# The last part of a decoder layer's down projection: the plain products of the last 256 rows, computed with rows on partitions instead of output features

## The chip, the cores and the metric

The kernel runs on one core of one Trainium2 chip. The metric is the device time of one execution in microseconds (us), the median of three runs. The matrix engine is PE, its weight loads are PEld, the vector engine is DVE, the scalar engine ACT, and SP issues the DMA transfers.

## The reference

One layer of a hybrid decoder is applied to 16 learned meta tokens and 512 prompt tokens, and to 8 separate sample tokens, with a model width D of 2048: a combined projection, windowed attention beside causal pooling, an output projection, a layer normalisation, a SwiGLU feed-forward part and a second normalisation. All inputs and outputs are float32. The change lies in the last three lines of it:

```python
def post_sublayers(h, attn_out, pool_out, w_o, ln1_g, ln1_b, w_gate, w_up, w_down, ln2_g, ln2_b):
    ...
    h1 = layer_norm(DEEPNORM_ALPHA * h + mix, ln1_g, ln1_b)
    a = jax.nn.silu(jnp.einsum('btd,df->btf', h1, w_gate)) * jnp.einsum('btd,df->btf', h1, w_up)
    ff = jnp.einsum('btf,fd->btd', a, w_down)
    return layer_norm(DEEPNORM_ALPHA * h1 + ff, ln2_g, ln2_b)
```

Here d_ff is 44 tiles of 128, and the normalisation takes mean and variance over the 2048 features of a token. The 8 sample rows and the 512 prompt rows are outputs; the meta rows are dropped.

## The kernel before, in words

*Layout.* A token is called a row here, as in the reference. Almost everywhere the kernel keeps features on the 128 partitions and tokens as columns. The sum alpha * h1 + ff thus stands in 16 tiles `acc[m]` of 128 features, each with 520 columns: 8 sample rows, then 512 prompt rows. At the very end it must be turned round, as a normalisation over the 2048 features of a row needs a row on one partition, and as the output is stored by rows.

*Arithmetic.* A float32 number is split into a rounded part and the rest, both in the type fp32r (`split`: ACT makes the high part in L187, DVE the low part in L188). Of each pair of operands PE makes three products (`products`, L203, L204 and L206: high by high, high by low, low by high). `rr` is the region of memory of such parts, `fr` that of float32 tiles. In a product the left operand is the stationary one (a tile of 128x128, loaded by PEld) and the right one moves through it column by column.

*The down projection.* Most of the 44 d_ff tiles go through a scheme of seven products instead of eight for pairs of blocks (`column_pair`); their sums stand in PSUM tiles `tri` and are added to `acc` by DVE (L1243 to L1256). Four d_ff tiles (f = 0 to 3, called `places`) are left out of that scheme and are done plainly at the end by `down(h, m)`. That is the stage the change touches. Its hidden activations are kept split as `ah[f]` and `al_[f]`, 128 features by 520 columns. For half h = 0 (264 columns: the sample rows and 256 prompt rows), and then for h = 1 (256 columns: the last 256 prompt rows), and for each of 16 output tiles m, there are 4 x 3 products with a 128x128 piece of w_down stationary and the columns moving, into a bank `d`; DVE adds the bank to `acc[m]` (L1336). So there are 192 products a half. The weights come in four loads of 4 tiles m (L1328, two buffers `pl`), and are split once for each m, with all four f side by side, 512 columns.

*Turning and normalising.* The 512 prompt rows are four blocks of 128, `Rows` 0 to 3; blocks 0 and 1 belong to the first half, 2 and 3 to the second. After every fourth m, `Rows.part(q)` turns 4 tiles of each block of the half by PE transposes with an identity matrix (L1350) into a bank `tz`, four to a bank: 16 banks and 64 transposes for the four blocks. ACT copies the bank to a tile `z` (L1352), and DVE takes statistics of its 512 features (L1354). After four parts, `Rows.end` aggregates them (L250), makes one over the standard deviation (`rstd_of`, L236 to L242, with the root on ACT in L237), and makes for each quarter q a centring pass (L1361: subtract the mean, times the weight) and a scaling pass (L1363: times one over the deviation, plus the bias), each over 128x512 on DVE. The scaled quarter is stored (L1364). The passes of blocks 0 and 1 are issued among the products of the second half; those of blocks 2 and 3 come after all of PE's products.

*The sample rows* are normalised without turning, by `sample_rows`, a generator advanced at fixed places: `tg` turns the norm's weights (L1378), column sums are made by products with a matrix of ones (L1392, tiles `zm` and `zv`), DVE scales (L1401 to L1403), and one last transpose `to` (L1406) brings the 8 x 16 pieces into rows, which ACT copies (L1408) and 16 small DMAs store (L1411).

*What sets the order.* A tile scheduler puts the instructions of each engine into one fixed order by the order of the program and by what its own model says of readiness; rings of buffers (8 PSUM banks, the `pl` and `z` buffers) hold steps back. `step()` pins the order of the instructions inside it. At run time every engine works through its own list in order, so an instruction that waits holds all behind it on that engine.

Of the kernel before, what the change touches and what calls it, by code (L numbers as in the profile page):

```python
# [8 lines left out]
F32 = mybir.dt.float32  # L9
F32R = mybir.dt.float32r  # L10
AF = mybir.ActivationFunctionType
ALU = mybir.AluOpType
AX = mybir.AxisListType

P = 128
D = 2048
KT = D // P
SEQ = 512
META = 16
NS = 8  # L20
# [29 lines left out]
NZ = 19  # L50
# [17 lines left out]
def hybrid_step(ctx, tc, xin, w_in, w_o, w_g, w_u, w_d, w_pool, par_d, cst_d, ident_d, ln2gb, kct_d, vc_d, hist_d,  # L68
                ck_d, cv_d, sp_d, yp, ys, nkp, nvp, npp, nks, nvs, nps):
    nc = tc.nc  # L70
# [744 lines left out]
    def bank(name, w=HN):  # L815
        return ps.tile([P, 512], F32, tag="bank", name=name, bufs=banks)[:, :w]
# [490 lines left out]
    plp = Pool(fr)  # L1307
# [6 lines left out]
    pw, ws = {}, {}  # L1314
# [8 lines left out]
    def down(h, m):  # L1323

        if m % 4 == 0 and h == 0:
            pw[h] = plp.tile([P, 4, 4, P], F32, tag="pl", name=f"pl{h}_{m}", bufs=2)
            for f, (c, x) in enumerate(places):
                nc.sync.dma_start(pw[h][:, :, f, :], w_d[c, m:m + 4, :, x * P:(x + 1) * P].rearrange("m p c -> p m c"))  # L1328
        hs = DHALF[h]
        out = bank(f"d{h}_{m}", hs.stop - hs.start)  # L1330
        if h == 0:
            ws[m] = split(pw[h][:, m % 4], f"dp{m}")
        wh, wl = ws[m]
        for f in range(4):
            products([out], wh[:, f, :], wl[:, f, :], [ah[f][:, hs]], [al_[f][:, hs]], f == 0, f == 3)
        nc.vector.tensor_add(acc[m][:, hs], acc[m][:, hs], out)  # L1336
# [4 lines left out]
    class Rows:  # L1341
        def __init__(self, c0, n, dst):
            self.c0, self.n, self.dst, self.z = c0, n, dst, []
            self.st, self.mv = stats_tile(pb, f"z{c0}")

        def part(self, q):
            n, c0 = self.n, self.c0
            tp = bank(f"tz{c0}_{q}", 512)
            for i in range(4):
                nc.tensor.transpose(tp[:n, i * P:(i + 1) * P], acc[4 * q + i][:, c0:c0 + n], ident)  # L1350
            z = zp.tile([P, 512], F32, tag="z", name=f"z{c0}_{q}", bufs=NZ)[:n]
            nc.scalar.copy(z, tp[:n])  # L1352

            nc.vector.bn_stats(self.st[:n, q, :], tp[:n] if q == 3 else z)  # L1354
            self.z.append(z)

        def end(self):
            n = self.n
            mu, r = stats_end(pb, self.st, self.mv, n, f"z{self.c0}")
            for q, z in enumerate(self.z):  # L1360
                nc.vector.scalar_tensor_tensor(z, z, mu, gb[0][q][:n], op0=ALU.subtract, op1=ALU.mult)  # L1361
                yield
                nc.vector.scalar_tensor_tensor(z, z, r, gb[1][q][:n], op0=ALU.mult, op1=ALU.add)  # L1363
                nc.sync.dma_start(self.dst[:, q * 512:(q + 1) * 512], z)  # L1364
                yield
# [50 lines left out]
    rows = [Rows(NS + P * i, P, yp[P * i:P * (i + 1), :]) for i in range(4)]  # L1416
    for h, part in ((0, rows[:2]), (1, rows[2:])):
        for m in range(KT):
            down(h, m)
            if h == 1:  # L1420

                for _ in range(2 if m % 4 == 1 else 1):
                    next(ends, None)
            if h == 0 and m in (1, 2):
                for i, q in gb_loads[4 * m - 4:4 * m]:
                    nc.sync.dma_start(gb[i][q], ln2gb[i:i + 1, q * 512:(q + 1) * 512].to_broadcast([P, 512]))
            if m % 4 == 3:
                for x in part:
                    x.part(m // 4)
            if (h, m) in ((0, 4), (0, KT - 1), (1, 4), (1, 10), (1, KT - 1)):  # L1430
                next(sample)
        ends = chain.from_iterable([x.end() for x in part])
    for _ in ends:
        pass
# [90 lines left out]
```

## Time and profile before

| what | value |
|---|---|
| median of three runs | 1921.79 us (1921.46 to 1921.79) |
| the profiled execution, its own time | 1923.03 us |
| span of that execution, first to last instruction | 1921.2 us |
| busy share of the span: PE, DVE, ACT, POOL | 98%, 80%, 50%, 0% |
| mean granted PE clock | 0.993 |
| plain stage, 1844.92 to 1901.60 | 56.68 us |
| from the end of PE's last plain product to the end of the span | 19.60 us |

The profile is one execution on the core; times in it are microseconds from the first instruction. A row of a timeline gives start, duration, engine, line, operation, output and inputs, and how often the instruction repeats without a break; PE's instructions overlap, so that the distance between two starts, not the duration of one, says what a product costs. A row of a table by stage gives the stretch, its length, the busy time and number of instructions of PE, PEld, DVE, ACT and POOL in it, and then the granted PE clock (1.00 is full speed), the DMA engines' busy share and their GB/s. A row of the waits says which engine's instruction waited for which: us in all, how often, the longest. The chain of waits follows the work that ended last back to what released it.

### The profile page before, as it was taken

The numbers are of one execution on the slowest core, as the hardware profiler recorded it, in microseconds if no ns is written. First come the engines' busy times: TensorE is split into PE (matmuls) and PEld (weight loads), VectorE is DVE, ScalarE is ACT, GpSimd is POOL, SyncE is SP. The second block draws the span as 40 slices with busy tenths as digits, with TensorE's granted clock in tenths as the row PEclk, the third lists the DMA queues.
The fourth block names the chain that finished last, engine by engine and source line by source line (L and its number), as shares of the span: only waits on it lengthen the run. The fifth ranks groups of instructions, "written<-read, shape, count | busy, mean of one in ns | idle before, by whom it ended". The sixth has DMA issues, their size and how long they took to land.

```text
span 1921.2 us, 39215 instructions
## 1 busy us (share of the span) xinstructions
PE 1890.5 (98%) x15533; PEld 1862.9 (97%) x15533; DVE 1537.7 (80%) x2734; ACT 957.6 (50%) x1808; POOL 2.7 (0%) x9
## 2 busy tenths in 40 slices
PE   8999999999999999999999999999999999999996
PEld 8999999999989999999999999999999999999996
DVE  6666667768777988988898888888877888888878
ACT  6644445545654555555555555555555433434341
POOL 0000000000000000000000000000000000000000
PEclk9999999999999999999999999999999999999998
DMA  8722222665745455454545344453568655645332
GB/s 281 233 99 68 70 75 71 206 207 193 251 153 176 150 171 172 148 183 145 176 149 172 128 164 151 153 169 127 178 243 322 233 197 178 219 166 191 94 100 90
DMA packets 145240, 319.27 MB, mean 166 GB/s; under 512 B 14288, under 2 KB 66232, under 8 KB 144952
## 3 DMA queue, kind: packets, MB, share of 16 engines
q1 hardware_dynamic: 144480, 315.71, 49.6%
q8 instruction: 122, 2.00, 0.4%
q10 hardware_dynamic: 576, 1.05, 0.2%
q14 instruction: 62, 0.51, 0.1%
HBM read 265.22 MB, written 54.03 MB: 166 GB/s over the span
## 4 chain that ended last, share of the span: by engine, by line
PE 92%; DVE 3%; DMA 2%; ACT 2%; issue 1%; SPq 0%; DVEq 0%; ACTq 0%
PE p_g L203 8%; PE p_g L204 8%; PE p_g L206 8%; PE p_u L203 7%; PE p_u L206 7%; PE p_u L204 7%; PE tri L203 6%; PE tri L206 6%; PE tri L204 6%; PE o L203 3%; PE o L206 3%; PE o L204 3%; PE p_u L1003 2%; PE mm_u L203 2%; PE mm_u L206 2%; PE mm_u L204 2%
## 5 line engine op out<-in xcount | busy, mean ns | idle before, releaser
L187 ACT CAST rr<-fr 128x512 fp32r<-128x512 f32 (+1 forms) x1056 | 669.9, 644 | 738.3 <-DVE fr L196 151.5
L188 DVE TENSOR_TENSOR rr<-fr,rr 128x512 fp32r<-128x512 f32 (+1 forms) x1056 | 743.7, 715 | 244.2 <-ACT rr L187 233.8
L196 DVE TENSOR_TENSOR fr<-fr 128x1024 f32<-128x1024 f32 (+1 forms) x304 | 319.2, 1050 | 4.9 <-DMA fr<-in_w_g_dram 4.3
L203 PE MATMUL p_g<-rr 128*128 128x260 f32 x830 | 234.1, 283 | 0.0
L206 PE MATMUL p_g<-rr 128*128 128x260 f32 x830 | 230.2, 282 | 0.0
L204 PE MATMUL p_g<-rr 128*128 128x260 f32 x788 | 221.4, 282 | 0.0
L203 PE MATMUL p_u<-rr 128*128 128x260 f32 x770 | 217.8, 283 | 0.6 <-ACT fr L1044 0.6
L206 PE MATMUL p_u<-rr 128*128 128x260 f32 x770 | 214.7, 281 | 0.0
L204 PE MATMUL p_u<-rr 128*128 128x260 f32 x748 | 210.5, 282 | 0.0
L206 PE MATMUL tri<-rr 128*128 128x260 f32 x696 | 196.7, 283 | 1.8 <-DVE rr L188 1.8
L203 PE MATMUL tri<-rr 128*128 128x260 f32 x696 | 197.1, 283 | 0.8 <-ACT rr L187 0.8
L204 PE MATMUL tri<-rr 128*128 128x260 f32 x696 | 196.7, 283 | 0.0
L203 PEld LDWEIGHTS p_g<-rr 128*128 128x128 f32 x830 | 156.1, 188 | 0.0
L206 PEld LDWEIGHTS p_g<-rr 128*128 128x128 f32 x830 | 155.1, 189 | 0.0
L204 PEld LDWEIGHTS p_g<-rr 128*128 128x128 f32 x788 | 148.1, 188 | 0.0
L203 PEld LDWEIGHTS p_u<-rr 128*128 128x128 f32 x770 | 144.8, 188 | 0.8 <-ACT fr L1044 0.8
L203 PE MATMUL o<-rr 128*128 128x260 f32 x512 | 145.0, 284 | 0.3 <-ACT rr L187 0.3
L206 PEld LDWEIGHTS p_u<-rr 128*128 128x128 f32 x770 | 144.4, 189 | 0.0
L204 PE MATMUL o<-rr 128*128 128x260 f32 x512 | 144.0, 282 | 0.0
L206 PE MATMUL o<-rr 128*128 128x260 f32 x512 | 143.6, 282 | 0.2 <-DVE rr L188 0.2
L204 PEld LDWEIGHTS p_u<-rr 128*128 128x128 f32 x748 | 140.6, 188 | 0.0
L206 PEld LDWEIGHTS tri<-rr 128*128 128x128 f32 x696 | 131.3, 189 | 2.6 <-DVE rr L188 2.6
(320 smaller groups left out, 4563.2 us busy)
## 6 DMA issues: line engine op xcount, KB each, us to landing
fr<-in_w_u_dram SPq DMA_DIRECT2D x100, 512.0 KB
fr<-in_w_g_dram SPq DMA_DIRECT2D x90, 512.0 KB
fr<-in_w_d_dram SPq DMA_DIRECT2D x64, 640.0 KB
t_d<-fr SPq DMA_DIRECT2D x140, 260.0 KB
fr<-in_w_o_dram SPq DMA_DIRECT2D x64, 512.0 KB
fr<-in_w_in_dram SPq DMA_DIRECT2D x48, 512.0 KB
rr<-t_d SPq DMA_DIRECT2D x87, 260.0 KB
mid_b<-t_d SPq DMA_DIRECT2D x53, 260.0 KB
```

The lines of the kernel that those rows point to most:

```text
L187: nc.scalar.copy(wh, s)
L188: last_lo[0] = (lo or nc.vector).tensor_sub(wl, s, wh.bitcast(F32)).ins
L196: i = op(*args).ins
L203: nc.tensor.matmul(o, wh, hi[j], start=first, stop=False, skip_group_check=onto)
L204: nc.tensor.matmul(o, wh, lo[j], start=False, stop=False, skip_group_check=onto)
L206: nc.tensor.matmul(o, wl, hi[j], start=False, stop=last, skip_group_check=onto)
L1003: nc.tensor.matmul(bk, self.q(0, n - 1)[:, k * P:(k + 1) * P], z1[0][4 * (n - 1) + k // 2][:, k % 2, :], start=(k == 0), stop=(k == 7))
```

## The change

The first half keeps its form, but is done by four groups q of four output tiles: `load_plain(q)` loads the weights with f outermost, `down_first(q)` splits one f of a group at a time (512 weight columns, kept in `ws[q, f]`), fills four banks, and adds them to `acc` (L1342).

The second half is done the other way round. `Rows.part(q, onto=True)`, for blocks 2 and 3, first puts the four tiles of `acc` into the bank `tz` by four plain float32 products with the identity (L1357, the tile stationary and the identity moving, which turns it), and then lets 12 products add to the same bank: the block's 128 columns of `ah[f]` and `al_[f]` are stationary, and 512 split weight columns move. The result stands in the bank with rows on partitions. So the second half's 192 products of 256 columns become 96 of 512, its 32 transposes become 32 identity products, and its 16 adds go. Blocks 0 and 1 are transposed as before (L1359).

The closing of the rows is ordered anew. `close_rows` takes blocks 0 and 1 together (one chain of small operations for both), then block 2 alone; block 3 comes last, with DVE's order pinned by `step`: centre, then scale and centre in turn. The lines are now: copy L1365, statistics L1366, aggregate L1369, centring L1373, scaling L1377, store L1378. Of the sample rows the lines are L1401 (`tg`), L1415 (`zm`, `zv`), L1424 to L1426 (scaling), L1429 (`to`), L1431 (copy), L1434 (16 stores). The loads of the norm's weights (`gb`) are issued after the first group.

```diff
-    def down(h, m):
-        if m % 4 == 0 and h == 0:
-            pw[h] = plp.tile([P, 4, 4, P], F32, tag="pl", name=f"pl{h}_{m}", bufs=2)
+    def load_plain(q):
+        if q < 4:
+            pl[q] = plp.tile([P, 4, 4, P], F32, tag="pl", name=f"pl{q}", bufs=2)
             for f, (c, x) in enumerate(places):
-                nc.sync.dma_start(pw[h][:, :, f, :], w_d[c, m:m + 4, :, x * P:(x + 1) * P].rearrange("m p c -> p m c"))
-        hs = DHALF[h]
-        out = bank(f"d{h}_{m}", hs.stop - hs.start)
-        if h == 0:
-            ws[m] = split(pw[h][:, m % 4], f"dp{m}")
-        wh, wl = ws[m]
+                nc.sync.dma_start(pl[q][:, f], w_d[c, 4 * q:4 * q + 4, :, x * P:(x + 1) * P].rearrange("m p c -> p m c"))
+    def down_first(q):
+        hs = DHALF[0]
+        out = [bank(f"d{4 * q + i}", hs.stop) for i in range(4)]
         for f in range(4):
-            products([out], wh[:, f, :], wl[:, f, :], [ah[f][:, hs]], [al_[f][:, hs]], f == 0, f == 3)
-        nc.vector.tensor_add(acc[m][:, hs], acc[m][:, hs], out)
+            ws[q, f] = wh, wl = split(pl[q][:, f].rearrange("p m c -> p (m c)"), f"dp{q}_{f}")
+            for i in range(4):
+                sl = slice(i * P, (i + 1) * P)
+                products([out[i]], wh[:, sl], wl[:, sl], [ah[f][:, hs]], [al_[f][:, hs]], f == 0, f == 3)
+        for i in range(4):
+            a = acc[4 * q + i][:, hs]
+            nc.vector.tensor_add(a, a, out[i])
     gb = [[pb.tile([P, 512], F32, name=f"gb{i}_{q}") for q in range(4)] for i in range(2)]
     gb_loads = [(i, q) for i in range(2) for q in range(4)]
     class Rows:
-        def __init__(self, c0, n, dst):
-            self.c0, self.n, self.dst, self.z = c0, n, dst, []
-            self.st, self.mv = stats_tile(pb, f"z{c0}")
-        def part(self, q):
-            n, c0 = self.n, self.c0
-            tp = bank(f"tz{c0}_{q}", 512)
+        def __init__(self, c0, dst, mv):
+            self.cs, self.dst, self.z = slice(c0, c0 + P), dst, []
+            self.st, self.mv = pb.tile([P, 4, 6], F32, name=f"st_z{c0}"), mv
+        def part(self, q, onto=False):
+            tp = bank(f"tz{self.cs.start}_{q}", 512)
             for i in range(4):
-                nc.tensor.transpose(tp[:n, i * P:(i + 1) * P], acc[4 * q + i][:, c0:c0 + n], ident)
-            z = zp.tile([P, 512], F32, tag="z", name=f"z{c0}_{q}", bufs=NZ)[:n]
-            nc.scalar.copy(z, tp[:n])
-            nc.vector.bn_stats(self.st[:n, q, :], tp[:n] if q == 3 else z)
+                o, a = tp[:, i * P:(i + 1) * P], acc[4 * q + i][:, self.cs]
+                if onto:
+                    nc.tensor.matmul(o, a, ident, start=i == 0, stop=False, skip_group_check=True)
+                else:
+                    nc.tensor.transpose(o, a, ident)
+            if onto:
+                for f in range(4):
+                    products([tp], ah[f][:, self.cs], al_[f][:, self.cs], [ws[q, f][0]], [ws[q, f][1]], False, f == 3, True)
+            z = zp.tile([P, 512], F32, tag="z", name=f"z{self.cs.start}_{q}", bufs=NZ)
+            nc.scalar.copy(z, tp)
+            nc.vector.bn_stats(self.st[:, q, :], tp if q == 3 else z)
             self.z.append(z)
-        def end(self):
-            n = self.n
-            mu, r = stats_end(pb, self.st, self.mv, n, f"z{self.c0}")
-            for q, z in enumerate(self.z):
-                nc.vector.scalar_tensor_tensor(z, z, mu, gb[0][q][:n], op0=ALU.subtract, op1=ALU.mult)
+            if q == 3:
+                nc.vector.bn_aggr(self.mv, self.st.rearrange("p a b -> p (a b)"))
+        def centre(self, q):
+            z = self.z[q]
+            nc.vector.scalar_tensor_tensor(z, z, self.mv[:, 0:1], gb[0][q], op0=ALU.subtract, op1=ALU.mult)
+        def scale(self, q, r):
+            z = self.z[q]
+            nc.vector.scalar_tensor_tensor(z, z, r, gb[1][q], op0=ALU.mult, op1=ALU.add)
+            nc.sync.dma_start(self.dst[:, q * 512:(q + 1) * 512], z)
+    def close_rows(part, mv):
+        r = rstd_of(pb, mv[:, :, 1], P, f"z{part[0].cs.start}")
+        for q in range(4):
+            for i, x in enumerate(part):
+                x.centre(q)
                 yield
-                nc.vector.scalar_tensor_tensor(z, z, r, gb[1][q][:n], op0=ALU.mult, op1=ALU.add)
-                nc.sync.dma_start(self.dst[:, q * 512:(q + 1) * 512], z)
+                x.scale(q, r[:, i:i + 1])
                 yield
...
     sample = sample_rows()
     next(sample)
-    rows = [Rows(NS + P * i, P, yp[P * i:P * (i + 1), :]) for i in range(4)]
-    for h, part in ((0, rows[:2]), (1, rows[2:])):
-        for m in range(KT):
-            down(h, m)
-            if h == 1:
-                for _ in range(2 if m % 4 == 1 else 1):
-                    next(ends, None)
-            if h == 0 and m in (1, 2):
-                for i, q in gb_loads[4 * m - 4:4 * m]:
-                    nc.sync.dma_start(gb[i][q], ln2gb[i:i + 1, q * 512:(q + 1) * 512].to_broadcast([P, 512]))
-            if m % 4 == 3:
-                for x in part:
-                    x.part(m // 4)
-            if (h, m) in ((0, 4), (0, KT - 1), (1, 4), (1, 10), (1, KT - 1)):
-                next(sample)
-        ends = chain.from_iterable([x.end() for x in part])
-    for _ in ends:
-        pass
+    mvs = [pb.tile([P, 2, 2], F32, name="mv01"), pb.tile([P, 1, 2], F32, name="mv2"), pb.tile([P, 1, 2], F32, name="mv3")]
+    rows = [Rows(NS + P * i, yp[P * i:P * (i + 1), :], mvs[max(0, i - 1)][:, i if i < 2 else 0]) for i in range(4)]
+    for q in range(2):
+        load_plain(q)
+    for q in range(4):
+        down_first(q)
+        load_plain(q + 2)
+        if q == 0:
+            for i in range(2):
+                for k in range(4):
+                    nc.sync.dma_start(gb[i][k], ln2gb[i:i + 1, k * 512:(k + 1) * 512].to_broadcast([P, 512]))
+        else:
+            for x in rows[:2]:
+                x.part(q - 1)
+        if q == 1:
+            next(sample)
+    rows[2].part(0, True)
+    for x in rows[:2]:
+        x.part(3)
+    next(sample)
+    ends = close_rows(rows[:2], mvs[0])
+    for q in range(1, 4):
+        rows[2].part(q, True)
+        if q > 1:
+            next(sample)
+        for _ in range(4):
+            next(ends)
+    rows[3].part(0, True)
+    for _ in range(4):
+        next(ends)
+    ends = close_rows(rows[2:3], mvs[1])
+    for q in range(1, 4):
+        rows[3].part(q, True)
+        if q == 1:
+            next(sample)
+        for _ in range(3):
+            next(ends, None)
+    x, dve = rows[3], (nc.vector,)
+    with step(*dve):
+        r = rstd_of(pb, mvs[2][:, :, 1], P, "z3")
+        x.centre(0)
+    for q in range(4):
+        with step(*dve):
+            if q:
+                x.centre(q)
+        with step(*dve):
+            x.scale(q, r)
 # ---- launch: one core; the arrays are laid out for the loads, the values are those that come in ----
```

*PE at its end.* The rows of PE's list before, from the last transposes to the end; `tz_2` and `tz_3` are the banks of quarters 2 and 3, `to` is the sample rows' bank.

```order
L1350 MATMUL tz_2_20720<-fr 128x128 [waits DVE_49]
L1350 MATMUL tz_2_20727<-fr 128x128
L1350 MATMUL tz_3_20792<-fr 128x128 [waits DVE_49]
L1350 MATMUL tz_3_20799<-fr 128x128
...
L1406 MATMUL to<-fr 128x128 [waits DVE_49,PE_49]
L1521 UNCONDITIONAL_BRANCH
```

And the same place after:

```order
L203 MATMUL tz_1_20615<-rr 128x512
L204 MATMUL tz_1_20615<-rr 128x512
L206 MATMUL tz_1_20615<-rr 128x512
L1429 MATMUL to<-fr 128x128 [waits DVE_49,PE_49]
L1357 MATMUL tz_2_20664<-fr 128x128 [waits PE_49]
L1357 MATMUL tz_2_20664<-fr 128x128 x3
L203 MATMUL tz_2_20664<-rr 128x512
L204 MATMUL tz_2_20664<-rr 128x512
```

`to` was PE's last instruction; now parts 2 and 3 of block 3, four identity products and twelve products each, stand behind it.

*DVE at the sample rows' last step.* The three scaling operations that `to` needs (L1401 to L1403 before, L1424 to L1426 after) and what stands among and behind them, before:

```order
L1401 TENSOR_TENSOR fr<-fr 128x128 [waits DVE_49]
L1354 BN_STATS fr<-tz_3_20792 128x6 [waits Activation_49]
L1354 BN_STATS fr<-tz_3_20799 128x6 [waits Activation_49]
L1402 TENSOR_TENSOR fr<-fr 128x128 [waits DVE_49]
L250 BN_AGGR fr<-fr 128x2 [waits DVE_49] x2
L1403 TENSOR_TENSOR fr<-fr 128x128 [waits DVE_49]
L236 TENSOR_SCALAR fr<-fr 128x1 [waits DVE_49]
L1361 SCALAR_TENSOR_TENSOR mid_c<-mid_c,fr 128x512 x4
```

And after:

```order
L1424 TENSOR_TENSOR fr<-fr 128x128 [waits DVE_49]
L1377 SCALAR_TENSOR_TENSOR mid_c<-mid_c,fr 128x512 [waits DVE_49]
L1377 SCALAR_TENSOR_TENSOR mid_c<-mid_c,fr 128x512 x3
L1425 TENSOR_TENSOR fr<-fr 128x128 [waits DVE_49]
L1426 TENSOR_TENSOR fr<-fr 128x128 [waits DVE_49]
L1366 BN_STATS fr<-mid_c 128x6 [waits Activation_49]
L1366 BN_STATS fr<-tz_3_20688 128x6 [waits Activation_49]
```

Before, the 16 passes of blocks 0 and 1 stood ahead of these operations, and those of blocks 2 and 3 behind; now the 24 passes of blocks 0, 1 and 2 stand ahead, the last four of them in the rows shown, and block 3's last statistics behind.

*DVE at the start of the stage.* The add L1256 ends the seven-product scheme. Before, adds of the plain sums stood ahead of it among the splits L188:

```order
L1253 TENSOR_TENSOR fr<-fr,tri_7_19964 128x520
L188 TENSOR_TENSOR rr<-fr,rr 128x512 [waits Activation_49]
L1336 TENSOR_TENSOR fr<-fr,d_2_20161 128x264 [waits PE_49]
L1336 TENSOR_TENSOR fr<-fr,d_0_20125 128x264 [waits PE_49]
L188 TENSOR_TENSOR rr<-fr,rr 128x512 [waits PE_49]
L188 TENSOR_TENSOR rr<-fr,rr 128x512 [waits Activation_49]
L1256 TENSOR_TENSOR fr<-fr,tri_7_19964 128x520 [waits PE_49]
```

After, the splits of the second group stand ahead of it and of the first group's adds:

```order
L1253 TENSOR_TENSOR fr<-fr,tri_7_19964 128x520
L188 TENSOR_TENSOR rr<-fr,rr 128x512 [waits DMAHW4_49,Activation_49]
L188 TENSOR_TENSOR rr<-fr,rr 128x512 [waits DMAHW3_49,Activation_49]
L188 TENSOR_TENSOR rr<-fr,rr 128x512 [waits DMAHW4_49,Activation_49]
L188 TENSOR_TENSOR rr<-fr,rr 128x512 [waits DMAHW5_49,PE_49]
L188 TENSOR_TENSOR rr<-fr,rr 128x512 [waits DMAHW2_49,Activation_49]
L188 TENSOR_TENSOR rr<-fr,rr 128x512 [waits DMAHW7_49,Activation_49]
L1256 TENSOR_TENSOR fr<-fr,tri_7_19964 128x520 [waits PE_49]
```

Before, the adds of two banks came between three splits; now six splits and no add stand there, and each of the six waits for a load as well.

More of the change, by code (lines that the diff above doesn't have):

```diff
@@ L1313, in hybrid_step @@
     places = [x for i in PLAIN for x in PLAIN[i]]
-    pw, ws = {}, {}
+    pl, ws = {}, {}
     sp[0].close()
```

## The prediction
> **What bounds the kernel now.** I read the page first, then busy time by stage, then the chain of waits and the engines' timelines over the last 80 us.
>
> ```profile
> span 1921.2 us, 39215 instructions
> PE 1890.5 (98%) x15533; PEld 1862.9 (97%) x15533; DVE 1537.7 (80%) x2734; ACT 957.6 (50%) x1808; POOL 2.7 (0%) x9
> PE 92%; DVE 3%; DMA 2%; ACT 2%; issue 1%; SPq 0%; DVEq 0%; ACTq 0%
> ```
>
> PE carries the kernel, but the change touches only its end. The busy times there, split at PE's last plain product:
>
> ```profile
> 1844.92:1901.60 56.68, 56.51 (x474) 56.06 (x473) 42.44 (x97) 17.68 (x40) 0.00 (x0) 1.00 0.32 98
> 1901.60:1921.20 19.60, 1.67 (x13) 1.16 (x11) 15.67 (x41) 2.73 (x7) 0.00 (x0) 0.60 0.31 111
> ```
>
> The columns are the length, then PE, PEld, DVE and ACT busy, then the granted clock. For 56.7 us PE is full (DVE 42.4); then come 19.6 us in which DVE alone sets the pace. The chain says what of:
>
> ```profile
> 1901.61 0.13 PE d L206
> 1901.76 0.42 DVE fr L1336
> ...
> 1905.94 2.65 DVE mid_c L1361 x4
> ...
> 1913.52 3.98 DVE mid_c L1363 x6
> ```
>
> The last sum is added (L1336), then two row blocks of 128 are normalised: 16 passes of 512 (L1361, L1363). So there are two currencies: PE time before 1901.6, DVE time behind it.
>
> **The change on PE.** Rates from the timeline, first and last row of unbroken runs (12, 18 and 13 steps), and ten transposes:
>
> ```profile
> 1859.68 0.29 PE L206 MATMUL d<-rr 128*128 128x264 f32 x1
> ...
> 1861.14 0.28 PE L206 MATMUL d<-rr 128*128 128x264 f32 x1
> ...
> 1895.82 0.28 PE L203 MATMUL d<-rr 128*128 128x256 f32 x1
> ...
> 1897.95 0.28 PE L203 MATMUL d<-rr 128*128 128x256 f32 x1
> ...
> 1901.57 1.25 PE L1350 MATMUL tz<-fr 128*128 128x128 f32 x10
> ```
>
> ```profile
> 20.43 0.29 PE L203 MATMUL kv<-rr 128*128 128x276 f32 x1
> ...
> 22.07 0.29 PE L204 MATMUL kv<-rr 128*128 128x276 f32 x1
> 1883.96 0.22 PE zm L1392 x2
> ```
>
> A product of 264 columns takes 0.122 us, of 256 0.118, of 276 0.126; a transpose (1.25 - 0.27) / 9 = 0.109; a plain fp32 product of 128 columns 0.22, being two instructions (the zm row is the chain's). A 512-column product is not in this trace. If each column beyond 256 costs what the rows of 256 and 276 show, 0.0004 us, it takes 0.22; twice a 256-column one is 0.236. I take 0.224, as the slope comes from rows of the same kind.
>
> Removed: 192 products x 0.118 = 22.7 and 32 transposes x 0.109 = 3.5. Added: 96 x 0.224 = 21.5 (up to 22.7) and 32 identity products x 0.22 = 7.0. PE gains 2.3 us of work (1.9 to 3.5). A part, four identity products and twelve of 512, costs 0.9 + 2.7 = 3.6.
>
> The 16 adds of 256 columns and eight of the 16 last passes leave DVE's end. If nothing else moved, PE would end 2.3 us later and the tail would shrink by more, a gain of a few us. But the order moves the sample rows' transpose `to`: it was PE's last instruction, and now PE's last two parts of rows 3 stand behind it, while on DVE 24 passes stand ahead of what it waits for. Its wait now:
>
> ```profile
> DVE rr L188 <- ACT rr L187: 4.9, 2, 4.3
> PE to L1406 <- DVE fr L236: 3.2, 1, 3.2
> PE tri L203 <- DVE fr L1248: 0.6, 1, 0.6
> ```
>
> Those 3.2 us cost nothing now, as no product follows. So I follow the new chain forward.
>
> *PE to the last transposes of rows 0 and 1.* The first plain product starts where it did, 1844.92. Behind it stand 27 products of the last column pair and 192 of the first half at 0.122 (26.7), 33 transposes (3.6) and one part (3.6): 1878.8. In the first plain groups the moved splits come ahead of DVE's add L1256, which frees PE's banks. That wait lies between nothing and the 4.3 us that DVE once waited for a split; PE's nearest own row shows 0.6, and I take 1.0. So 1879.8.
>
> *DVE from there to L1426.* The two copies on ACT (0.6 each, partly beside the transposes) put bn_stats 1.3 us later, 1881.1. Then, in order, DVE has 6 bn_stats, 24 passes and 27 small operations until the sample rows are ready.
>
> ```profile
> 1903.96 1.29 DVE L1354 BATCH_NORM_STATS2 fr<-tz 128x6 f32<-128x512 f32 x2
> ...
> 1911.35 0.27 DVE L239 TENSOR_TENSOR fr<-fr 128x1 f32<-128x1 f32 x2
> 1911.54 0.28 DVE L240 TENSOR_TENSOR fr<-fr 128x1 f32<-128x1 f32 x2
> ...
> 1912.11 5.38 DVE L1363 SCALAR_TENSOR_TENSOR mid_c<-mid_c,fr 128x512 f32<-128x512 f32 x8
> ```
>
> A bn_stats follows the next after 0.60, a pass after (5.38 - 0.74) / 7 = 0.66; small operations 0.09 each in pairs, 0.19 where one waits for the other, 0.14 in the middle. Sum 3.6 + 15.9 + 3.8 = 23.3, hence 1904.4. PE meanwhile does five parts and the two small sample sums (18.0 + 0.4) and stands at `to` from 1898.2. It waits 6.2 us there (5 to 7).
>
> *The rest.* `to` and two parts, 0.2 + 7.2: 1911.8 at full clock. Copy and last bn_stats start 0.9 later; bn_stats 0.7, aggregate 0.25, L236 0.14, a centring pass 0.66 (it covers the root on ACT) and five steps of 0.19 bring the first scaling to 1915.4. The step order pairs the passes: each scaling must see its centring end (0.74 and some 0.05), so 4 x 0.66 + 3 x 0.79 + 0.1 = 5.1, to 1920.5. Now the last pass ends at 1917.5, 3.7 before the span does:
>
> ```profile
> 1915.70 2.16 SPq L1364 DMA_DIRECT2D out_dram<-mid_c  x4
> ```
>
> These four transfers queue 0.7 us apart; the new ones come 1.45 apart, so 3.5. Span 1924.0: 2.8 more than now, at full clock.
>
> *The clock.* It stays full only while PE works. Columns as above:
>
> ```profile
> 294.53:297.94 3.41, 3.41 (x32) 3.03 (x30) 3.41 (x18) 0.85 (x4) 0.00 (x0) 1.00 0.28 101
> 297.94:301.35 3.41, 3.41 (x17) 3.41 (x18) 3.34 (x14) 3.41 (x16) 0.00 (x0) 0.50 0.63 167
> 301.35:304.77 3.42, 3.42 (x17) 3.42 (x17) 1.59 (x7) 1.03 (x6) 0.00 (x0) 0.50 0.38 140
> 304.77:308.18 3.41, 3.41 (x30) 3.41 (x29) 0.69 (x1) 0.79 (x2) 0.00 (x0) 1.00 0.17 41
> 1902.21:1905.62 3.41, 0.61 (x6) 0.37 (x4) 3.35 (x11) 1.72 (x4) 0.00 (x0) 1.00 0.00 0
> 1905.62:1909.03 3.41, 0.45 (x1) 0.18 (x1) 3.41 (x9) 0.67 (x3) 0.00 (x0) 0.50 0.02 5
> ```
>
> After a stretch of 3.41 us with PE idle but for 0.61, the next is granted 0.50, and it took two such stretches (17 products each, against 30) to come back at 304.77. A wait of 6.2 us leaves a stretch nearly empty however it falls, so the two last parts start at half clock. That lasts between 2.8 and 6.1 us and loses half of it, 1.4 to 3.1; I take 2.3. Span 1926.3, 5.1 more than now. The Trainium skill, "TensorE: Matmul & The Clock Gate", Part 1, says the same as a rule against long PE gaps: an idle window of about 3.4 us halves the clock, and a busy one restores it. By that rule the loss is my 1.4 to 3.1; the trace agrees in the rows above.
>
> The profiled execution took 1923.03 us against a median of 1921.79; I add the 5.1 us to the median: **1926.9 us**. About 0.2% (3.8 us) is what a measurement of this kernel can tell from no change.
>
> **Rivals.**
> - *The clock holds* (the other side: not slower). The place is the wait at `to`; if the stretches fall so that none counts as idle, or the wait is under some 3 us, nothing is lost after it: +2.8, 1924.6. It decides below a loss of 1.0 us. Against it stands the 0.50 row behind a wait of only 3.2 us. Chance 0.17.
> - *No wait at `to`*, if DVE's queue runs some 6 us ahead of my sum. Then PE ends parts at 1905.6 instead of 1911.8, and full clock holds: 2.8 - 6.2 = -3.4, 1918.4, and with no wait at the start 1917.4. For it speaks that DVE is idle a quarter of the stage now; against it, that its passes there stand at 0.66 without a pause. Chance 0.07.
> - *A 512-column product costs little more than a 256-column one.* At 0.131 us the start of DVE's sum comes 1.1 earlier and the last two parts are 2.2 shorter: +1.8, 1923.6. The same page of the Trainium skill, "Back-to-back issue gap", gives 131 ns sustained for N=512, beside 216 ns alone. The 256-column row at 0.118 and the 276-column one at 0.126 speak against 0.131. Chance 0.04.
> - *The start waits longer.* If weight loads for the third and fourth group hold DVE by 4.3 instead of 1.0: +8.4, 1930.2. Chance 0.06.
>
> **How the numbers follow.** The forecast has 0.66. Its own range, from the bounds of start (0 to 2.5) and clock (1.4 to 3.1), is 1925.0 to 1929.2. To hold 8 in 10 the range reaches down through the clock rival with no wait at the start (1923.6, less 0.6 for DVE's small operations) and up to the late start: 1923.0 to 1930.0. Slower: 0.66 + 0.06, less 0.02 at the lower edge, 0.70. Within 0.2%: 0.17 + 0.04 + 0.02 and half of "no wait", 0.26. Faster: 0.04.
>
> **What would show it.** In the profile after: PE idle some 6 us before `to`, released by DVE; the two last parts at first with twice the spacing and a granted 0.50; 512-column products 0.22 apart; about 9 us from the last product to the last pass. I am wrong if PE runs through `to` without a wait, if the last parts run at full clock, or if the plain stage loses more than 2.5 us before its second group.

## The result, and the profile after

The changed kernel took 1927.97 us in the median of seven runs (1925.99 to 1929.16); the kernel before, run beside it, 1921.79 (seven runs). The ratio is 1.0036, with a 95% interval of 1.0027 to 1.0045: it is slower by 5 to 9 us. The profiled execution took 1926.95 us with a span of 1925.1.

The page's head and its chain that ended last, of the kernel after:

```profile
span 1925.1 us, 39072 instructions
PE 1895.4 (98%) x15469; PEld 1864.7 (97%) x15469; DVE 1534.2 (80%) x2712; ACT 958.4 (50%) x1807; POOL 2.7 (0%) x9
PE 92%; DMA 3%; DVE 3%; ACT 1%; issue 1%; SPq 0%; ACTq 0%; DVEq 0%
```

The shares read almost as before, so nothing can be learned from them; the stage must be cut up. The first plain product starts at 1843.22 here and at 1844.92 before. PE's list up to there is the same, and it took 1841.6 to 1844.9 us in the profiles of this study, so all lengths below count from each profile's own first plain product. The busy times by stretch, of the kernel after: to the product ahead of `to`, the wait, `to` with the last two parts, and what comes behind.

```profile
1843.22:1898.29 55.07, 53.45 (x379) 49.64 (x377) 40.14 (x81) 18.97 (x41) 0.00 (x0) 1.00 0.35 101
1898.29:1904.21 5.92, 0.16 (x2) 0.04 (x2) 5.74 (x19) 0.58 (x1) 0.00 (x0) 0.69 0.30 110
1904.21:1913.23 9.02, 9.02 (x41) 7.59 (x41) 0.69 (x1) 0.85 (x2) 0.00 (x0) 0.82 0.16 52
1913.23:1925.10 11.87, 0.15 (x1) 0.00 (x0) 7.48 (x16) 0.79 (x2) 0.00 (x0) 0.69 0.23 88
```

The stretch behind PE's last product fell from 19.6 to 11.9 us: block 3 alone is closed there. But PE is through with its last product 70.0 us behind the start of the first plain one (1913.23 - 1843.22, where 1913.23 is one spacing of 0.23 behind the last product's start) instead of 56.7, and the whole is 81.9 instead of 76.3. In the second row PE does next to nothing (0.16 of 5.92 us) while DVE is busy for 5.74: the wait. Its end on PE's timeline, with the wait and what released it in brackets:

```profile
1898.06 0.39 PE L206 MATMUL tz<-rr 128*128 128x512 f32 x1
1904.21 0.45 PE L1429 MATMUL to<-fr 128*128 128x128 f32 x1 [5.76 <-DVE fr L1426]
1904.45 1.92 PE L1357 MATMUL tz<-fr 128*128 128x128 f32 x8
1906.02 0.77 PE L203 MATMUL tz<-rr 128*128 128x512 f32 x1
1906.59 0.63 PE L204 MATMUL tz<-rr 128*128 128x512 f32 x1
1907.02 0.58 PE L206 MATMUL tz<-rr 128*128 128x512 f32 x1
1907.44 0.40 PE L203 MATMUL tz<-rr 128*128 128x512 f32 x1
1907.67 0.39 PE L204 MATMUL tz<-rr 128*128 128x512 f32 x1
```

Behind the wait the products stand 0.43 us apart, then, from 1907.44, 0.23. On DVE, the operations on both sides of it: the last passes of block 2, the sample rows' last steps, and the next thing DVE has to do.

```profile
1900.80 2.73 DVE L1377 SCALAR_TENSOR_TENSOR mid_c<-mid_c,fr 128x512 f32<-128x512 f32 x4
1903.45 0.28 DVE L1425 TENSOR_TENSOR fr<-fr 128x128 f32<-128x128 f32 x1
1903.77 0.29 DVE L1426 TENSOR_TENSOR fr<-fr 128x128 f32<-128x128 f32 x1
1910.36 0.69 DVE L1366 BATCH_NORM_STATS2 fr<-mid_c 128x6 f32<-128x512 f32 x1 [6.29 <-ACT mid_c L1365]
...
1921.12 0.75 DVE L1377 SCALAR_TENSOR_TENSOR mid_c<-mid_c,fr 128x512 f32<-128x512 f32 x1
```

So the two engines wait for each other in turn: PE 5.8 us for DVE's list, and then DVE 6.3 us for the part that PE could have done meanwhile. The granted clock in the stretches of 3.41 us that the profile shows around the wait (columns as in the prediction):

```profile
1897.17:1900.59 3.42, 1.27 (x6) 0.71 (x4) 3.42 (x16) 0.58 (x1) 0.00 (x0) 1.00 0.01 3
1900.59:1904.00 3.41, 0.00 (x0) 0.00 (x0) 3.38 (x8) 0.00 (x0) 0.00 (x0) 0.50 0.45 165
1904.00:1907.42 3.42, 3.21 (x12) 2.98 (x13) 0.06 (x1) 0.27 (x1) 0.00 (x0) 0.50 0.42 150
1907.42:1910.83 3.41, 3.41 (x20) 2.94 (x19) 0.47 (x1) 0.58 (x1) 0.00 (x0) 1.00 0.06 12
```

From 1904.45 to 1907.42 PE worked at half clock and lost half of those 3.0 us, 1.5. The start of the stage has two waits:

```profile
1846.68 0.76 PE L206 MATMUL d<-rr 128*128 128x264 f32 x4 [0.75 <-DVE rr L188]
1851.10 0.76 PE L206 MATMUL d<-rr 128*128 128x264 f32 x4 [0.87 <-DVE rr L188]
```

From one product's start to the next it is 1.04 and 1.15 us there instead of 0.12, so 1.95 us are lost. What stands ahead of the second wait, on ACT and then on DVE:

```profile
1849.09 1.14 ACT L187 CAST rr<-fr 128x512 fp32r<-128x512 f32 x2 [0.45 <-DMA fr<-in_w_d_dram]
1849.75 1.90 DVE L188 TENSOR_TENSOR rr<-fr,rr 128x512 fp32r<-128x512 f32 x3 [0.38 <-ACT rr L187]
```

ACT waits for a load, and the first of DVE's three splits waits for ACT. By the program's list that first split is of the fourth group's weights; PE waits for the second of the three, one of the first group, which only stands behind it. The six splits ahead of the add L1256 thus belong to all four groups and not to the second alone.

### The profile page after: what moved, and what is told of

The parts are those of the page before. It is cut to its first block, busy times and chain, and to the rows that moved or that the text cites. A ratio compares the mean times of both kernels' runs of the same rounds, so it can differ in the third digit from the quotient of the medians.

```text
span 1925.1 us, 39072 instructions
## 1 busy us (share of the span) xinstructions
PE 1895.4 (98%) x15469; PEld 1864.7 (97%) x15469; DVE 1534.2 (80%) x2712; ACT 958.4 (50%) x1807; POOL 2.7 (0%) x9
## 4 chain that ended last, share of the span: by engine, by line
PE 92%; DMA 3%; DVE 3%; ACT 1%; issue 1%; SPq 0%; ACTq 0%; DVEq 0%
PE p_g L203 8%; PE p_g L204 8%; PE p_g L206 8%; PE p_u L203 7%; PE p_u L206 7%; PE p_u L204 7%; PE tri L203 6%; PE tri L206 6%; PE tri L204 6%; PE o L203 3%; PE o L206 3%; PE o L204 3%; PE p_u L1003 2%; PE mm_u L203 2%; PE mm_u L206 2%; PE mm_q L203 2%
## 5 line engine op out<-in xcount | busy, mean ns | idle before, releaser
L188 DVE TENSOR_TENSOR rr<-fr,rr 128x512 fp32r<-128x512 f32 (+1 forms) x1056 | 745.5, 717 | 241.1 <-ACT rr L187 230.6
```

What stands on the lines that cost most here:

```text
L188: last_lo[0] = (lo or nc.vector).tensor_sub(wl, s, wh.bitcast(F32)).ins
```

## The experiments

*Theory A*, that of the prediction: PE's wait at `to` and the half clock behind it lie on the path, and so do the waits at the start; without them the change would gain. *Theory B*: DVE's own list sets the end; PE's wait lies beside it and costs nothing. *Theory C*, against one part of A: the products behind the wait are slow for some other reason than PE's idleness. *Theory D*, against another: the weights' loads land when their buffers let them start, whatever queues beside them.

All runs are measured against the kernel before, which ran beside them (medians of 1921.8, 1920.6, 1921.1 and 1920.5 us on the four occasions, so that ratios can be compared and times less well); the lengths come from one profile each.

| run | ratio, 95% interval | first plain product to the start of the last product | to the end of the last pass | to the end of the span |
|---|---|---|---|---|
| before | 1 | 56.5 | 72.6 | 76.3 |
| the change | 1.0036 (1.0027 to 1.0045) | 69.8 | 78.7 | 81.9 |
| `to` last | 0.9997 (0.9989 to 1.0006) | 63.3 | 72.1 | 75.8 |
| PE kept at work | 1.0024 (1.0015 to 1.0034) | 67.9 | 76.8 | 80.1 |
| norm's weights late | 1.0031 (1.0019 to 1.0042) | 69.3 | 78.1 | 81.4 |
| `to` last, transposes | 0.9990 (0.9981 to 0.9999) | 58.7 | 69.0 | 73.3 |
| sample sums sooner | 1.0007 (0.9998 to 1.0016) | 66.2 | 75.0 | 78.3 |
| both edits | 0.9991 (0.9982 to 1.0000) | 61.0 | 69.9 | 73.6 |
| both, 256 columns | 0.9993 (0.9985 to 1.0002) | 61.9 | 70.7 | 74.3 |
| four edits | 0.9990 (0.9981 to 0.9999) | 62.4 | 70.2 | 74.5 |
| four, stores pinned | 0.9990 (0.9981 to 0.9999) | 62.1 | 70.0 | 73.8 |

### `to` last

```diff
         rows[3].part(q, True)
-        if q == 1:
-            next(sample)
         for _ in range(3):
             next(ends, None)
+    next(sample)
```

> The sample rows' last transpose `to` is issued behind block 3's parts, so that no product stands behind it on PE; nothing else changes. Theory A (PE waits at `to` for DVE's queue, and the wait and the half clock behind it lie on the path): the wait of 5.9 us and the 1.7 us lost at half clock go, so PE's last product ends some 7.6 us earlier, and DVE, which is through with the sample rows at about that time, follows at once: 1927.97 - 7.6 = 1920.4 us, between 1919.4 and 1921.4. Theory B (DVE's own list sets the end, and PE's wait lies beside it): less than 2 us gained, 1926 or more.

Measured: 1920.19 us, 0.9997 (0.9989 to 1.0006). The end of the last product's stretch and of DVE's list, in this run's profile:

```profile
1905.05 0.40 PE L206 MATMUL tz<-rr 128*128 128x512 f32 x1
1905.28 0.27 PE L1429 MATMUL to<-fr 128*128 128x128 f32 x1
```

```profile
1903.88 0.28 DVE L1426 TENSOR_TENSOR fr<-fr 128x128 f32<-128x128 f32 x1
1906.10 0.70 DVE L1366 BATCH_NORM_STATS2 fr<-tz 128x6 f32<-128x512 f32 x1 [1.94 <-ACT mid_c L1365]
...
1913.18 0.75 DVE L1377 SCALAR_TENSOR_TENSOR mid_c<-mid_c,fr 128x512 f32<-128x512 f32 x1
```

PE runs through all its parts at 0.23 us a product, DVE ends the sample rows 1.1 us before PE's last product does, and waits 1.9 us for it instead of 6.3 and 3.0. The last pass comes 6.5 us sooner than with the change, although the second wait at the start was 1.1 us longer in this execution (2.26 us between two products instead of 1.15); so 7.6 without that, as A had it. Theory B has fallen. This one step in the wrong place was the whole of the loss, as far as the ratios can tell.

### PE kept at work

```diff
-        to = bank("to", P)
-        nc.tensor.transpose(to, flat(z), ident)
+        to = bank("to", 512)
+        with step(nc.tensor):
+            for _ in range(24):
+                nc.tensor.matmul(to, ah[0][:, 8:136], ws[0, 0][0], start=True, stop=True)
+            nc.tensor.transpose(to[:, :P], flat(z), ident)
+        to = to[:, :P]
```

> 24 extra products of 512 columns into `to`'s own bank are put ahead of `to` on PE (24 x 0.233 = 5.6 us of work whose result is overwritten), so that PE works while it would wait; the order is otherwise that of the changed kernel. Theory A: `to` starts when it did, its wait falls from 5.9 to some 0.3 us, the granted clock stays at 1.00, and the last two parts run at 0.22 an identity product and 0.233 a product from the first: 1.7 us less, 1926.3 us (1925.3 to 1927.0). Theory C (the slow products behind the wait are slow for another reason than PE's idleness): no change, 1928.0, and the first parts behind `to` still at 0.43.

Measured: 1924.74 us, 1.0024 (1.0015 to 1.0034). The scheduler did not keep the order: it put the real transpose into the last part (1908.71), so that the 24 products stand in the place of the wait and the two parts follow them at once, 0.6 us sooner than with the change. The busy times of the filled stretch and of the two parts behind, in this run:

```profile
1898.03:1903.43 5.40, 5.40 (x25) 4.33 (x24) 5.37 (x19) 0.59 (x1) 0.00 (x0) 1.00 0.26 97
1903.43:1910.90 7.47, 7.47 (x42) 6.17 (x40) 0.87 (x2) 0.85 (x2) 0.00 (x0) 1.00 0.20 73
```

The clock is 1.00 throughout. From the first identity product behind the stretch to the start of the last product it is 7.2 us (1903.43 to 1910.68) instead of 8.5 with the change (1904.45 to 1912.99): 1.3 us, by the clock alone. With the 0.6 that makes the 1.9 us by which the last pass is sooner. Theory C has fallen. A's 1.7 for the clock was a little high. The time lies below A's range of 1925.3 to 1927.0; the kernel before ran 1.2 us faster on that occasion, too, and by the ratios the run is 2.3 us below the change.

### The norm's weights late

```diff
-                nc.sync.dma_start(pl[q][:, f], ...)
+                with step(nc.sync):
+                    nc.sync.dma_start(pl[q][:, f], ...)
...
-        if q == 0:
+        if q == 2:
             for i in range(2):
                 for k in range(4):
-                    nc.sync.dma_start(gb[i][k], ...)
+                    with step(nc.sync):
+                        nc.sync.dma_start(gb[i][k], ...)
-        else:
+        if q:
```

> The eight loads of the norm's weights are pinned on SP behind all loads of the plain weights; nothing else changes. Theory A (the start of the plain stage waits for the third group's weights, which queue with those loads): the weights land about 1 us sooner, the second of the two waits at the start (1.0 us) goes, the first (0.9 us, for a buffer that PE itself frees) stays: 1927.0 us (1926.0 to 1927.6). Theory D (the loads start when their buffer comes free, and that alone sets the wait): both waits stay, 1928.0.

Measured: 1926.54 us, 1.0031 (1.0019 to 1.0042), which by itself can't be told from the change's 1.0036. The profile can: of the two waits at the start one is left.

```profile
1847.52 0.75 PE L206 MATMUL d<-rr 128*128 128x264 f32 x4 [0.74 <-DVE rr L188]
```

So the second wait is gone, as A had it, and D, by which both would stay, missed. The profiles agree: the wait is there in all five with the loads in their old place (0.9 to 2.0 us) and in none of the five with them late. But which part of the edit took it away is not shown. The edit also pins the order of the plain weights' loads, and with that the scheduler orders the splits anew: in the program's list of DVE, the first group's split that PE waited for no longer stands behind the two of the fourth group. The new order alone could do it, without any load landing sooner. Why the whole gained only 0.5 us in its profile shows in the clock behind the wait at `to`, which starts at 1903.83 in this run:

```profile
1898.35:1901.76 3.41, 0.00 (x0) 0.00 (x0) 3.41 (x15) 0.34 (x1) 0.00 (x0) 1.00 0.00 0
1901.76:1905.18 3.42, 1.35 (x7) 1.38 (x8) 1.89 (x5) 0.27 (x1) 0.00 (x0) 0.50 0.86 309
1905.18:1908.59 3.41, 3.41 (x11) 2.83 (x11) 0.00 (x0) 0.00 (x0) 0.00 (x0) 0.50 0.05 11
1908.59:1912.00 3.41, 3.41 (x20) 2.92 (x20) 0.69 (x1) 0.59 (x1) 0.00 (x0) 1.00 0.04 8
```

Here a stretch's border falls into the first of the two parts. The stretch with 1.35 us of work doesn't bring the clock back, and PE works at half clock for 4.8 us instead of 3.0: 2.4 lost instead of 1.5. Where the borders fall against the wait thus moves the time by about 1 us.

### `to` last, and transposes

```diff
-                if onto:
-                    nc.tensor.matmul(o, a, ident, start=i == 0, stop=False, skip_group_check=True)
-                else:
-                    nc.tensor.transpose(o, a, ident)
+                nc.tensor.transpose(o, a, ident)
```

> As with `to` behind block 3's parts, and the 32 identity products are transposes again, onto which the products add. PE saves 32 x 0.11 = 3.5 us. Theory A: then DVE's list, not PE, sets the start of block 3's last statistics (DVE ends the sample rows at 1904.06, PE would end some 2 us before that), so only about 2 of the 3.5 us show: 1918.5 us (1917.5 to 1919.4). Rival: PE sets the end still, 3.5 us less than with `to` last, 1916.9; or the transposes don't lie on the path at all, 1920.4.

The output of this run lacks, as far as is known, part of the sums that the transposes bring into the banks of blocks 2 and 3, so it counts for its time alone. Measured: 1918.68 us, 0.9990 (0.9981 to 0.9999). PE's last product starts 4.5 us sooner than with `to` last, of which 0.9 is a shorter wait at the start: 3.6, the price of the identity products over transposes. The last pass is 3.1 us sooner, 2.2 without the start's share. DVE's list holds the rest back, as A had it.

### Sample sums sooner

```diff
         rows[2].part(q, True)
-        if q > 1:
+        if q < 3:
             next(sample)
```

> The sample rows' sums are issued one part of block 2 sooner; `to` stays where the change put it, ahead of block 3's last two parts. On DVE L1426 now stands ahead of the four scaling passes of block 2 (2.65 us) instead of behind them. Theory A: PE's wait at `to` falls from 5.9 to some 3 us (less by what PE then waits at `zv`, 0 to 1.6); a wait that short leaves no stretch of 3.41 us empty, so the clock holds too: 2.8 + 1.7 = 4.5 us less than the changed kernel, 1.0036 - 0.0023 = 1.0013 of the kernel before; with the clock lost all the same 1.0021. Theory B (the wait lies beside DVE's list and costs nothing): 1.0036.

Measured: 1922.8 us, 1.0007 (0.9998 to 1.0016). `to` and the granted clock around it:

```profile
1901.05 0.30 PE L1429 MATMUL to<-fr 128*128 128x128 f32 x1 [1.76 <-DVE fr L241]
```

```profile
1894.65:1898.06 3.41, 3.41 (x21) 2.94 (x20) 3.40 (x10) 0.69 (x2) 0.00 (x0) 1.00 0.66 202
1898.06:1901.48 3.42, 1.66 (x10) 1.13 (x9) 2.84 (x12) 0.68 (x2) 0.00 (x0) 1.00 0.00 0
1901.48:1904.89 3.41, 3.41 (x20) 2.89 (x20) 2.45 (x4) 0.17 (x1) 0.00 (x0) 1.00 0.41 152
```

The row names L241 as the releaser, a step of block 2 that stands right behind L1426 on DVE; L1426 ends at 1900.91. PE's wait at `to` is 1.8 us instead of 5.8 (and `zv` waits 1.3), the clock stays at 1.00, and 3.6 us are gained in the profile, 2.9 thousandths in the ratio, somewhat more than A forecast (2.3): with `to` in its old place, its price goes with what stands ahead of it on DVE. That is theory A again, by the other engine.

### Both edits; and 256 columns

The edits of `to` last and of the norm's weights late together:

> Both edits that gave something: `to` behind block 3's parts, and the eight loads of the norm's weights behind the plain weights. With `to` last alone it was 0.9997 of the kernel before. Theory A: the second wait at the start goes (1.0 us with the changed kernel, 2.0 in the profile with `to` last): 0.9997 - 0.0008 = 0.9989, about 1919.7 us (1918.7 to 1920.2). Rival: DVE's list, not PE, sets the end once `to` is last: no change, 0.9997.

Measured: 1919.24 us, 0.9991 (0.9982 to 1.0000); by the ratio that can't be told from `to` last alone. In the profile the last pass is 2.2 us sooner, of which the start gave nearly all: its second wait, 2.1 us in that execution, is gone.

And on top of it, each product of 512 columns as two of 256:

```diff
-                    products([tp], ah[f][:, self.cs], al_[f][:, self.cs], [ws[q, f][0]], [ws[q, f][1]], False, f == 3, True)
+                    products([tp[:, x:x + 256] for x in (0, 256)], ah[f][:, self.cs], al_[f][:, self.cs],
+                             *[[w[:, x:x + 256] for x in (0, 256)] for w in ws[q, f]], False, f == 3, True)
```

> As the run with both edits, but each product of 512 columns is two of 256 into the halves of the bank, so 192 of 256 columns. Theory A: a product costs by its columns, 192 x 0.118 against 96 x 0.233, 22.7 against 22.4: 0.3 us more, 0.9991 of the kernel before. Rival (the wide products themselves carry the gain, each instruction having a cost of its own): 2 us or more, 1.0000 or above.

Measured: 1920.03 us, 0.9993 (0.9985 to 1.0002), not to be told from the run before it. In the profiles the starts of two parts, first of this run, then with 512 columns:

```profile
1897.47 1.05 PE L1358 MATMUL tz<-fr 128*128 128x128 f32 x8
1901.20 1.05 PE L1358 MATMUL tz<-fr 128*128 128x128 f32 x8
```

```profile
1896.95 1.05 PE L1358 MATMUL tz<-fr 128*128 128x128 f32 x8
1900.63 1.05 PE L1358 MATMUL tz<-fr 128*128 128x128 f32 x8
```

A part takes 3.73 us against 3.68, so 0.4 us over eight parts. The width of the products is worth no more than that. What shows in the profiles instead is the tail: from the start of the last product to the end of the last pass it is 16.0 us before and 8.9 with the change, with `to` last and with both edits.

### Four edits, and the stores pinned

```diff
-            nc.scalar.copy(z, tp)
-            nc.vector.bn_stats(self.st[:, q, :], tp if q == 3 else z)
+            if q == 3:
+                nc.vector.bn_stats(self.st[:, q, :], tp)
+            nc.scalar.copy(z, tp)
+            if q < 3:
+                nc.vector.bn_stats(self.st[:, q, :], z)
...
-    x, dve = rows[3], (nc.vector,)
...
+    for _ in close_rows(rows[3:], mvs[2]):
+        pass
```

> As the run with both edits, and in each block's last part the statistics read the bank ahead of ACT's copy instead of behind it, and block 3 is closed in the scheduler's own order (four centring passes, then four scaling ones) instead of the pinned pairs. Theory A: the chain behind PE's last product is the path: the copy's 0.6 us leaves it, and the passes follow each other at 0.66 without the pairs' pauses, 0.9 us less, of which the four stores, closer together, give back some 0.5: 1.0 us less than with both edits, 0.9984, about 1918.7 us (1917.9 to 1919.4). Rival: DVE's list ends no sooner than PE, so that the copy is hidden: 0.4 us at most, 0.9987.

> As the run with the four edits, and on SP the sample rows' 16 small stores are pinned ahead of block 3's four stores instead of running among and behind them. With the four edits the span ended 4.3 us after the last pass, five small stores being issued behind the first of the last two big ones; with the changed kernel, whose last issues are the four big stores, it ended 3.3 us after it. Theory A: the small stores are what ends last: some 1.0 us less, 0.9990 - 0.0005 = 0.9985 of the kernel before (0.9979 to 0.9989). Rival: the big stores, now behind the small ones, end last and no sooner: 0.9990.

Measured: 1919.24 us, 0.9990 (0.9981 to 0.9999), and with the small stores pinned ahead 1918.97, 0.9990 (0.9981 to 0.9999). Neither can be told from both edits alone. Block 3's end on DVE, in the second of the two:

```profile
1904.05 0.70 DVE L1367 BATCH_NORM_STATS2 fr<-tz 128x6 f32<-128x512 f32 x1 [1.34 <-PE tz L206]
...
1905.15 2.73 DVE L1377 SCALAR_TENSOR_TENSOR mid_c<-mid_c,fr 128x512 f32<-128x512 f32 x4
...
1908.76 2.74 DVE L1381 SCALAR_TENSOR_TENSOR mid_c<-mid_c,fr 128x512 f32<-128x512 f32 x4
```

The statistics now wait for PE and not for ACT, and from the start of the last product to the end of the last pass it is 7.9 us instead of 8.9: that worked. But PE's last product is 1.0 to 1.3 us later than with both edits, for a wait in the plain stage that both these profiles have and that of both edits has not: a product waits there for an add (L1343) that stands behind a split whose weights landed late, and on SP the norm's weights are issued right behind these. The order of DVE's splits and adds there is the same in the three kernels, and the two other profiles with the loads late (`to` in its old place, and 256 columns) have no such wait, so it looks like the transfers' own variation; that was not tried by itself. The pinned stores brought the end of the span from 4.3 to 3.9 us behind the last pass, not to 3.3: the small stores were less than half of it.

Four of these versions lie at 0.9990 to 0.9993. With `to` in its place the form that the change brings beats the kernel before by about 0.1%, at the edge of what can be told.

## Why the prediction was right

The mechanism was right, at the place named, with its two follow-ups, and the median (1926.9 forecast, 1927.97 measured) lies in the range. Counted from the first plain product, forecast and measured (the forecast's times less 1844.92):

- *PE's products.* A 512-column product was taken at 0.224 us and takes 0.233: the bound by doubling (0.236) was nearer than the slope between 256 and 276 columns. That is 0.9 us over 96, but only three of the eight parts lie on the path (0.3 us); the others run beside DVE's list. The identity products were right at 0.22: a part of four of them and twelve products takes 3.68 us (1883.14 to 1886.82). PE's work grew by 96 x 0.233 + 32 x 0.22 - 26.2 = 3.2 us, not 2.3.
- *The start.* Taken at 1.0, bounds 0 and 2.5; it was 1.95. The engine was right (DVE's splits, the second time behind ones that wait for weights), the step was not: the prediction had PE wait for a bank that the add L1256 frees. PE waits twice, both times for a split itself, the first time for one that waits for PE in its turn.
- *The last transposes of blocks 0 and 1* ended at 36.4 instead of 34.9: the 0.95 of the start, and 0.6 that were not broken down.
- *From there to DVE's statistics.* Taken at 1.3 us for ACT's two copies, it was 0.4 (1879.63 to 1880.02): the copies run beside the transposes and the statistics ahead.
- *DVE to L1426.* The sum of 23.3 us was 24.0 (1880.02 to 1904.06); L1426 ended at 60.8 instead of 59.5.
- *The wait at `to`.* Forecast 6.2 (5 to 7), measured 5.8; both of its ends were late by about the same.
- *The clock.* Forecast 2.3 (1.4 to 3.1); 1.5 in this profile and 2.4 in another. The bounds were right, and which value comes is a matter of where the stretches fall. None of the rival's cases came up: in both profiles with the long wait the clock was lost.
- *Behind the last product.* Forecast 8.7 us to the end of the last pass, measured 8.6 (1913.23 to 1921.87); then 3.5 forecast and 3.2 measured to the end of the span.

In sum 81.4 forecast and 81.9 measured, against 76.3 before. Along the path, the terms that were too small (start 0.95, the rest up to the last transposes 0.6, DVE's sum 0.7) and those that were too large (ACT's copies 0.9, clock 0.8) nearly cancel. So the mechanism was right, but that the sum comes within half a microsecond is in part luck. The remaining half microsecond to one of the median lies in the executions: those of the change spread over 3.2 us (1925.99 to 1929.16), the profiled one of them stood 1.0 below its median, and the profiled one of before 1.2 above.

The rival that there is no wait at `to`, if DVE were quicker, forecast 3.4 us less than before. The run with `to` last has the same order of PE's work without that wait, and shows 0.4 less in the profile: what was forecast, less the 0.9 of the products and some 2 of that execution's start (3.1 us in its two waits instead of 1.0).

## What to carry to other kernels

An instruction that belongs to a side job (here one transpose for 8 rows) costs nothing at the end of an in-order engine's list and everything that stands behind it when it is moved forward: look for the last instruction of the list before, and ask what a new order puts behind it and what its operands stand behind on the other engine. A wait of two engines for each other in turn shows as two idle times of like length, one after the other, while the shares of the page stay as they were. And count a loss of clock with each wait that leaves PE idle for most of a stretch. When an edit pins the order of one engine, look whether the scheduler has also changed that of another, or the run tests two things at once.

## What the runs showed of the hardware

How empty a stretch must be to cost the clock: stretches of 3.41 us with 0.00, 1.27 and, in the prediction's rows, 0.61 us of PE's work were followed by a granted 0.50, and one with 1.66 (sample sums sooner) by 1.00. One with 1.35 at half clock didn't bring the full clock back, one with 3.21 did. But no border in busy time fits all rows. Early in the kernel after:

```profile
16.43:19.84 3.41, 1.92 (x13) 1.37 (x11) 1.60 (x3) 2.56 (x6) 0.00 (x0) 1.00 1.04 377
19.84:23.26 3.42, 3.42 (x16) 3.39 (x15) 3.04 (x6) 3.42 (x7) 0.00 (x0) 0.50 1.05 394
```

Here 1.92 us of work, most of its instructions transposes, did not keep the clock that 1.66 kept. The Trainium skill, "TensorE: Matmul & The Clock Gate", Part 1, says that the clock drops after an idle window of about 3.4 us, that the window runs freely, and that a measured ramp varies with its phase. The profiles agree on the length and on the variation (1.5 and 2.4 us lost behind the same wait), but a window need not be empty: 1.27 us of work in it did not save it.

Nor is a full PE enough. In the prediction's first stretch with a granted 1.00 (294.53 to 297.94) PE counts as busy for all of 3.41 us, and the next is at 0.50 all the same. The largest group of PE's instructions in that stretch, and in the next, of the kernel before:

```profile
L697 PE MATMUL smT<-fr 128*128 128x8 f32 x24 | 2.9, 260 | 0.0
...
L697 PE MATMUL smT<-fr 128*128 128x8 f32 x10 | 2.1, 347 | 0.0
```

These are small instructions of 8 moving columns. So the busy time of the profile isn't what the clock goes by. That few columns count for little would fit these rows; no run tests it. The prediction read those rows as two stretches of products at half clock before it came back; the first of the two still held ten of these small ones, and the other, full of products, sufficed, as did one stretch behind the wait at `to` (1904.00 to 1907.42).

The products of this kernel cost by their columns: 0.118 us for 256, 0.233 for 512. The same page, "Back-to-back issue gap", gives 131 ns for 512 columns in a sustained stream, beside some 216 in isolation; the stream here measures 233, and the measurement decides.
